# Idle matmuls on TensorE, a nested loop, a later pause with an earlier release, and another order and cut of the first loads

## The chip, the cores and the metric

One core of one Trainium2 chip runs the kernel. The metric is the device time of one execution in microseconds; three executions of the kernel before gave 162.36, 162.41 and 163.22 us, and the median, 162.41 us, is what the change is measured against. The kernel is compiled once for the fixed shapes below.

## The reference

A linear layer with a low-rank addition. x is 16 x 2048 rows of 256 floats, 32,768 rows or 33.55 MB; W is 256 x 256, lora_A 256 x 16, lora_B 16 x 256, lora_E 16 values, all fp32; the output is as large as x.

```python
x_flat = x.reshape(-1, in_dim)
y = x_flat @ W
lora_out = x_flat @ lora_A
lora_out = lora_out * lora_E
lora_out = lora_out @ lora_B
y = y + scale * lora_out
return y.reshape(batch, seq_len, out_dim).astype(np.float32)
```

## The kernel before

The small matrices are folded first: weff = W + A diag(E) B scale, in bf16, so that each row of x needs one product with weff. For this TensorE transposes lora_A against an identity that GpSimd writes (L125, L127, L153), VectorE (DVE) scales it into `ate` (L157), TensorE multiplies it with lora_B (L162), and DVE adds W and rounds (L167).

The rows of x go through the core in six chunks of `PLAN` = 48, 32, 48, 48, 48 and 32 rows per partition (128 partitions; one row per partition is 128 KiB in all, so a chunk is 6 or 4 MiB). The chunks lie in four slots of on-chip memory: chunk 4 goes into the slot of chunk 0, chunk 5 into that of chunk 1. The result is written over the chunk's input in the same slot, and stored from there.

A step is 8 rows per partition; there are NS = 32 steps: steps 0 to 5 are chunk 0, 6 to 9 chunk 1, 10 to 15 chunk 2, 16 to 21 chunk 3, 22 to 27 chunk 4 and 28 to 31 chunk 5. Each step goes through these stages, with two buffers each:

- `rounded(t)`, DVE (L141): rounds the 8 rows to bf16 into `xb`. It first waits for the chunk's load, where the step begins a piece of it.
- `transposed`, TensorE (L180): eight transposes, each of two bf16 columns at once as one fp32 word, into `ps_xt`.
- `copied(t)`, DVE (L145): copies `ps_xt` to `xt`.
- `multiplied`, TensorE (L191): 16 matmuls with weff in two halves of eight, into `ps_y[0]` and `ps_y[1]`.
- ScalarE (L214): copies each half from `ps_y` into the slot. The last half of a chunk releases the chunk's store.

DVE's order is rounded(0), the addition of weff, rounded(1), and then copied(t), rounded(t+2) for each t. TensorE's order is a loop over pairs of steps: transposed(t+1), multiplied(t). So the matmuls of a step stand behind the transposes of the next.

All large transfers are issued by SP in one queue, in this order: chunk 0's first 16 rows, W, chunk 0's other 32 rows (`PIECES`), chunk 1, chunk 2 in two pieces of 24 rows, chunk 3; then store 0 and store 1 when their chunks are computed; load 4 after store 0 has landed; load 5 after store 1 has landed (`AFTER`, L224 to L227); then stores 2, 3, 4 and 5, each when its chunk is computed. ScalarE issues the three small loads (lora_A, lora_B, lora_E).

There is one deliberate pause: `HOLD = {3: 1}` makes DVE wait, before it rounds the first step of chunk 3 (step 16), until store 1 has landed (L136 to L140).

Of the kernel before, what the change touches and what calls it, by code (L numbers as in the profile page):

```python
# [3 lines left out]

PLAN = [48, 32, 48, 48, 48, 32]

PIECES = {0: [16, 32], 2: [24, 24]}

SLOTS = [48, 32, 48, 48]
LEAD = 4  # L10
AFTER = {1: [4, 5]}

HOLD = {3: 1}

S, G = 8, 4
P = 128
# [17 lines left out]
def kernel(tc, x, W, lora_A, lora_B, lora_E, scale, out):  # L34
    nc = tc.nc
# [8 lines left out]

    steps = [(i, r) for i, b in enumerate(PLAN) for r in range(0, b, S)]
    NS = len(steps)
    assert NS % 2 == 0

    def rows_of(flat, i):
        b, r0 = PLAN[i], starts[i]  # L50
        return flat[r0:r0 + b * P, :].rearrange("(p b) k -> p b k", b=b)

    def sbuf(name, shape, dt):
        return nc.alloc_sbuf_tensor(name, shape, dt).ap()

    def psum(name, shape, dt):
        return nc.alloc_psum_tensor(name, shape, dt).ap()
# [7 lines left out]
    ate = sbuf("ate", [R, KC, P], BF16)  # L65
    weff = sbuf("weff", [P, KC, M], BF16)
    ident = sbuf("ident", [P, P], FP32)

    xb = [sbuf(f"xb{k}", [P, S, K], BF16) for k in range(2)]
    words = [t[:, :, :].rearrange("p s k -> p (s k)").bitcast(FP32).rearrange("p (s w) -> p s w", s=S) for t in xb]  # L70
# [4 lines left out]
    ps_y = [psum(f"psum_y{k}", [P, G, M], FP32) for k in range(2)]  # L75
# [4 lines left out]
    s_w, s_a, s_b, s_e = (Count(nc, f"s_{k}") for k in "wabe")  # L80

    pieces = {}
    for i, b in enumerate(PLAN):
        parts = PIECES.get(i, [b])
        pieces[i] = [(sum(parts[:j]), n) for j, n in enumerate(parts)]
    s_ld = {(i, r): Count(nc, f"s_ld{i}_{r}") for i in pieces for r, n in pieces[i]}
    s_st = [Count(nc, f"s_st{i}") for i in range(len(PLAN))]
    s_id, s_set, s_v, s_t, s_m, s_y = (
        Count(nc, k) for k in ("s_id", "s_set", "s_v", "s_t", "s_m", "s_y"))


    can_m = nc.alloc_semaphore("can_m")
# [1 line left out]
    can_y = [[nc.alloc_semaphore(f"can_y{h}_{k}") for k in range(2)] for h in range(S // G)]  # L94

    def slot(i):
        return slots[i % LEAD][:, :PLAN[i], :]

    def load(i, parts=None):
        for r, n in parts or pieces[i]:  # L100
            s_ld[i, r].by(nc.sync.dma_start(out=slot(i)[:, r:r + n, :], in_=rows_of(x_flat, i)[:, r:r + n, :]), 16)
# [4 lines left out]
    def spent(engine, count):  # L106
        engine.wait_ge(count.sem, count.total).then_inc(count.sem, -count.total)

    def take(sem):
        nc.tensor.wait_ge(sem, 1).then_inc(sem, -1)  # L110


    with tc.tile_critical(no_gpsimd_drain=True):
        load(0, pieces[0][:1])
        s_w.by(nc.sync.dma_start(out=w_sb, in_=W.rearrange("(p c) m -> p c m", c=KC)), 16)
        s_a.by(nc.scalar.dma_start(out=a_sb, in_=lora_A.rearrange("(p c) r -> p c r", c=KC)), 16)
        s_b.by(nc.scalar.dma_start(out=b_sb, in_=lora_B), 16)
        s_e.by(nc.scalar.dma_start(out=e_sb, in_=lora_E[:, None]), 16)
        load(0, pieces[0][1:])
        for i in range(1, LEAD):  # L120
            load(i)
    tc.close()
# [9 lines left out]
    def rounded(t):  # L132
        i, r = steps[t]
        if (i, r) in s_ld:
            nc.vector.wait_ge(s_ld[i, r].sem, 16)
        if i in HOLD and r == 0:  # L136

            for _ in range(10):
                nc.vector.engine_nop()
            nc.vector.wait_ge(s_st[HOLD[i]].sem, 16)  # L140
        nc.vector.tensor_copy(out=xb[t % 2], in_=slot(i)[:, r:r + S, :]).then_inc(can_t[t % 2], 1)  # L141

    def copied(t):
        nc.vector.wait_ge(s_t.sem, t + 1)
        nc.vector.tensor_copy(out=xt[t % 2], in_=ps_xt[t % 2]).then_inc(can_m, 1)  # L145


    nc.vector.wait_ge(s_b.sem, 16)
# [3 lines left out]
    for c in range(KC):  # L152
# [4 lines left out]
    s_v.by(nc.vector.tensor_scalar(  # L157
        out=ate, in0=ps_at, scalar1=e_sb, scalar2=float(scale),
        op0=mybir.AluOpType.mult, op1=mybir.AluOpType.mult))
    nc.tensor.wait_ge(s_v.sem, 2)  # L160
    for c in range(KC):
        aeb_done = nc.tensor.matmul(ps_aeb[:, c, :], ate[:, c, :], b_bf, start=True, stop=True)  # L162
    s_set.by(aeb_done)
    rounded(0)
    nc.vector.wait_ge(s_w.sem, 16)
    nc.vector.wait_ge(s_set.sem, 2)
    s_v.by(nc.vector.tensor_add(out=weff, in0=w_sb, in1=ps_aeb))  # L167
    rounded(1)
    for t in range(NS):
        copied(t)  # L170
        if t + 2 < NS:
            rounded(t + 2)

    nc.vector.sem_inc(can_t[NS % 2], 1)


    def transposed(k):
        nc.tensor.wait_ge(can_t[k], 1)
        for j in range(S):
            done = nc.tensor.transpose(ps_xt[k][:, j, :], words[k][:, j, :], ident)  # L180
            if j == 1:
                done.then_inc(can_t[k], -1)
        done.then_inc(s_t.sem, 1)

    def multiplied(k):
        take(can_m)
        for h in range(S // G):
            nc.tensor.wait_ge(can_y[h][k], 1)
            for j in range(G):
                for c in range(KC):  # L190
                    done = nc.tensor.matmul(  # L191
                        ps_y[h][:, j, :], pairs[k][:, h * G + j, :, c], weff[:, c, :],
                        start=(c == 0), stop=(c == KC - 1))
                if j == 0:
                    done.then_inc(can_y[h][k], -1)
            done.then_inc(s_m.sem, 1)

    transposed(0)
    nc.tensor.wait_ge(s_v.sem, 3)

    with nc.tensor.Fori(0, NS // 2):
        for k in range(2):
            transposed(1 - k)
            multiplied(k)
    s_t.total, s_m.total = NS + 1, NS * S // G

    for h in range(S // G):
# [1 line left out]
    n = 0  # L209
    for i, r in [(i, r + g) for i, r in steps for g in range(0, S, G)]:  # L210
        n += 1
        nc.scalar.wait_ge(s_m.sem, n)
        t, h = divmod(n - 1, S // G)
# [16 lines left out]
    for count in [s_a, s_id]:  # L230
        spent(nc.tensor, count)
    spent(nc.tensor, s_v)
    for count in [s_b, s_e, s_w, s_set, s_t] + list(s_ld.values()):
        spent(nc.vector, count)
    spent(nc.scalar, s_m)
    nc.tensor.wait_ge(can_y[0][NS % 2], 1).then_inc(can_y[0][NS % 2], -1)
# [37 lines left out]
```

## Time and profile before

| | us |
|---|---|
| median of three executions | 162.41 |
| the profiled execution | 162.57 |
| its span, first to last instruction | 161.3 |
| TensorE matmul busy | 93.2 |
| VectorE busy | 76.6 |
| ScalarE busy | 63.2 |
| mean granted TensorE clock | 0.822 of full |

An execution is 1.3 us longer than the span, which runs from the first to the last instruction that was profiled. Busy time of the compute engines counts their instructions alone. The DMA share is the mean busy share of the core's 16 DMA engines; in short windows it can pass 1.00, because a packet of up to 48 KiB is put down to the window in which it falls. The granted clock was 1.00 from the start to 22 us, about 0.5 for 3.4 us from there, 1.00 until 63 us, 0.50 through the pause and up to 90 us, 1.00 until 134.7 us, and 0.50 from then to the end, when TensorE has nothing more to do.

The pause is easy to find in the trace: ScalarE's last copy before it ends near 60.8 us, and DVE's first rounding after it begins at 83.4 us. At the start DVE rounds two steps at 9.6 and 11.3 us and then waits 5.5 us for the second piece of chunk 0, until 19.6 us. Issues to landing: chunk 0's first piece 8.4 us, W 8.5 us, the stores 28.0 to 36.5 us.

### The profile page before, as it was taken

Reading aid. Unit: us, or ns where it says so; the run is one execution under the profiler, and the core shown is the slowest. Engines: PE = TensorE matmul, PEld = TensorE weight load, DVE = VectorE, ACT = ScalarE, POOL = GpSimd, SP = SyncE. Lnnn points to the kernel's source line nnn. Section 1 sums busy time; section 2 is a strip of 40 time slices with the busy share of each in tenths; the row PEclk is TensorE's granted clock in tenths of the full one; section 3 lists DMA queues with packets and bytes.
Section 4 is the critical chain, followed back from the end, with each engine's and each line's share of the span. In section 5 each row is a group of like instructions: output and inputs, shape, how many; then the busy total and the mean of one; then the engine's idle time right before and its main releaser. Section 6 shows DMA issues by size and latency. Waiting matters only on the chain.

```text
span 161.3 us, 1875 instructions
## 1 busy us (share of the span) xinstructions
PE 93.2 (58%) x780; PEld 83.4 (52%) x780; DVE 76.6 (48%) x67; ACT 63.2 (39%) x65; POOL 0.7 (0%) x6
## 2 busy tenths in 40 slices
PE   0149179999999980000009999999999970000000
PEld 0038058999999960000008899999999960000000
DVE  0074197898989800000039589898989500000000
ACT  0300406777768680000000577776868680000000
POOL 0100000000000000000000000000000000000000
PEclk9999978999999998555555899999999997555555
DMA  4999999999999999989999989999999999999993
GB/s 137 407 496 423 423 423 433 408 463 408 506 439 427 402 390 392 500 386 398 480 435 402 500 378 406 471 431 404 463 463 415 402 451 463 427 402 402 447 447 171
DMA packets 2370, 67.42 MB, mean 418 GB/s; under 512 B 432, under 2 KB 448, under 8 KB 576
## 3 DMA queue, kind: packets, MB, share of 16 engines
q1 hardware_dynamic: 2160, 67.37, 97.7%
q10 hardware_dynamic: 208, 0.03, 0.1%
q14 instruction: 2, 0.02, 0.0%
HBM read 33.85 MB, written 33.55 MB: 418 GB/s over the span
## 4 chain that ended last, share of the span: by engine, by line
PE 44%; DMA 22%; ACT 2%; DVE 1%; issue 0%
PE psum_y L191 29%; DMA out_dram<-xy 22%; PE psum_xt L180 14%; ACT xy L214 2%; DVE xb L141 1%
## 5 line engine op out<-in xcount | busy, mean ns | idle before, releaser
L214 ACT COPY xy<-psum_y 128x1024 f32<-128x1024 f32 x64 | 61.9, 1015 | 64.0 <-PE psum_y L191 64.0
L191 PE MATMUL psum_y<-weff,xt 128*128 128x256 bf16 x512 | 64.9, 283 | 0.1
L191 PEld LDWEIGHTS psum_y<-weff,xt 128*128 128x128 bf16 x512 | 51.8, 101 | 7.6 <-issue 0.3
L141 DVE CAST xb<-xy 128x2048 bf16<-128x2048 f32 x32 | 39.0, 1217 | 32.3 <-DMA out_dram<-xy 26.8
L180 PE MATMUL psum_xt<-ident,xb 128*128 128x128 f32 x264 | 37.1, 288 | 29.7 <-DVE xb L141 29.7
L180 PEld LDWEIGHTS psum_xt<-ident,xb 128*128 128x128 f32 x264 | 32.3, 150 | 31.3 <-DVE xb L141 30.9
L145 DVE COPY xt<-psum_xt 128x1024 f32<-128x1024 f32 x32 | 39.2, 1224 | 11.2 <-PE psum_xt L180 11.2
L153 PE MATMUL psum_xt<-ident,a_sb 128*16 128x128 f32 x2 | 0.6, 397 | 6.8 <-POOL ident L127 6.8
L149 DVE CAST b_bf<-b_sb 16x256 bf16<-16x256 f32 x1 | 0.3, 281 | 7.9 <-DMA b_sb<-in_lora_B_dram 7.9
L214 ACT ACT_TABLE_LOAD x1 | 1.3, 1283 | 6.0 <-PEq L123 6.0
L153 PEld LDWEIGHTS psum_xt<-ident,a_sb 128*16 128x16 f32 x2 | 0.1, 90 | 6.7 <-DMA a_sb<-in_lora_A_dram 6.7
L162 PE MATMUL psum_xt<-b_bf,ate 16*128 16x256 bf16 x2 | 0.6, 402 | 2.4 <-DVE ate L157 2.4
L162 PEld LDWEIGHTS psum_xt<-b_bf,ate 16*128 16x128 bf16 x2 | 0.1, 104 | 2.9 <-DVE ate L157 2.9
L157 DVE TENSOR_SCALAR ate<-psum_xt,e_sb 16x256 bf16<-16x256 f32 x1 | 0.5, 473 | 1.0 <-DMA e_sb<-in_lora_E_dram 1.0
L167 DVE TENSOR_TENSOR weff<-w_sb,psum_xt 128x512 bf16<-128x512 f32 x1 | 0.7, 669 | 0.0
L127 POOL TENSOR_SCALAR_AFFINE_SELECT ident<-ident 128x128 f32<-128x128 f32 x1 | 0.3, 292 | 0.2 <-POOL ident L125 0.2
L125 POOL MEMSET ident<- 128x128 f32 x1 | 0.2, 205 | 5.4 <-POOLq L123 5.4
L255 POOL MEMSET const-bfloat16-1.0<- 128x1 bf16 x1 | 0.1, 102 | 0.0
L255 POOL MEMSET const-uint8-127<- 128x1 uint8 x1 | 0.1, 101 | 0.0
L255 POOL MEMSET const-float32-0.0<- 128x1 f32 x1 | 0.1, 98 | 0.2 <-issue 0.2
L255 POOL MEMSET const-float32-1.0<- 128x1 f32 x1 | 0.1, 98 | 0.0
## 6 DMA issues: line engine op xcount, KB each, us to landing
out_dram<-xy SPq DMA_DIRECT2D x4, 6144.0 KB, 30.6
xy<-in_x_dram SPq DMA_DIRECT2D x3, 4096.0 KB, 24.5
xy<-in_x_dram SPq DMA_DIRECT2D x2, 6144.0 KB, 39.3
out_dram<-xy SPq DMA_DIRECT2D x2, 4096.0 KB, 31.8
xy<-in_x_dram SPq DMA_DIRECT2D x2, 3072.0 KB, 36.7
xy<-in_x_dram SPq DMA_DIRECT2D x1, 2048.0 KB, 8.4
w_sb<-in_W_dram SPq DMA_DIRECT2D x1, 256.0 KB, 8.5
a_sb<-in_lora_A_dram ACTq DMA_DIRECT2D x1, 16.0 KB, 5.7
```

The source lines that it names most:

```text
L127: s_id.by(nc.gpsimd.affine_select(out=ident, in_=ident, compare_op=mybir.AluOpType.not_equal, fill=1.0, base=0, pattern=[[-1, P]], channel ...
L141: nc.vector.tensor_copy(out=xb[t % 2], in_=slot(i)[:, r:r + S, :]).then_inc(can_t[t % 2], 1)
L145: nc.vector.tensor_copy(out=xt[t % 2], in_=ps_xt[t % 2]).then_inc(can_m, 1)
L149: s_v.by(nc.vector.tensor_copy(out=b_bf, in_=b_sb))
L153: at_done = nc.tensor.transpose(ps_at[:, c, :], a_sb[:, c, :], ident)
L157: s_v.by(nc.vector.tensor_scalar(out=ate, in0=ps_at, scalar1=e_sb, scalar2=float(scale), op0=mybir.AluOpType.mult, op1=mybir.AluOpType.mult))
L162: aeb_done = nc.tensor.matmul(ps_aeb[:, c, :], ate[:, c, :], b_bf, start=True, stop=True)
L167: s_v.by(nc.vector.tensor_add(out=weff, in0=w_sb, in1=ps_aeb))
L180: done = nc.tensor.transpose(ps_xt[k][:, j, :], words[k][:, j, :], ident)
L191: done = nc.tensor.matmul(ps_y[h][:, j, :], pairs[k][:, h * G + j, :, c], weff[:, c, :], start=(c == 0), stop=(c == KC - 1))
L214: y = nc.scalar.copy(out=slot(i)[:, r:r + G, :], in_=ps_y[h])
L255: nc = _bacc.Bacc("TRN2", target_bir_lowering=False, num_devices=1)
```

## The change

It has five parts.

- **Order of the first loads.** W is issued ahead of everything else on SP, and then all of chunk 0 (two pieces of 24 rows instead of 16 and 32, W between them no more).
- **Chunk 2** is loaded in one piece of 48 rows instead of two of 24.
- **DVE's order at the start.** The addition of weff comes ahead of rounded(0) instead of behind it.
- **The pause.** It stands one step later, ahead of rounded(17) (t = NS/2 + 1), and waits for store 0 instead of store 1. When store 0 has landed, DVE raises `go` and waits for `s_warm` before it goes on.
- **TensorE.** `idle(n)` issues n fp32 matmuls of the identity with itself repeated four times (512 columns) into `ps_y[0]`, whose result nobody reads: one behind the transposes of lora_A, two behind the matmuls of lora_B, and five at the end of each half of the steps. The loop is nested, two passes over 16 steps each; at the end of a pass TensorE takes `go`, waits until `ps_y[0]` is free, runs the five and raises `s_warm`. The second pass does so at the very end.

```diff
-PIECES = {0: [16, 32], 2: [24, 24]}
+PIECES = {0: [24, 24]}
-HOLD = {3: 1}
+HOLD = 0
+WARM = 1, 2, 5
...
+    wide = ident[:, :].unsqueeze(1).to_broadcast([P, 4, P])
...
     with tc.tile_critical(no_gpsimd_drain=True):
-        load(0, pieces[0][:1])
         s_w.by(nc.sync.dma_start(out=w_sb, in_=W.rearrange("(p c) m -> p c m", c=KC)), 16)
...
-        load(0, pieces[0][1:])
+        load(0)
...
-        if i in HOLD and r == 0:
+        if t == NS // 2 + 1:
 
             for _ in range(10):
                 nc.vector.engine_nop()
-            nc.vector.wait_ge(s_st[HOLD[i]].sem, 16)
+            nc.vector.wait_ge(s_st[HOLD].sem, 16)
+            nc.vector.sem_inc(go, 1)
+            nc.vector.wait_ge(s_warm.sem, 1)
...
+    def idle(n):
+
+        last = None
+        for _ in range(n):
+            last = nc.tensor.matmul(ps_y[0][:, :2, :].rearrange("p g m -> p (g m)"), ident, wide, start=True, stop=True)
+        return last
...
+    idle(WARM[0])
     nc.tensor.wait_ge(s_v.sem, 2)
...
-    rounded(0)
     nc.vector.wait_ge(s_w.sem, 16)
     nc.vector.wait_ge(s_set.sem, 2)
     s_v.by(nc.vector.tensor_add(out=weff, in0=w_sb, in1=ps_aeb))
+    rounded(0)
     rounded(1)
...
     nc.vector.sem_inc(can_t[NS % 2], 1)
+    nc.vector.sem_inc(go, 1)
...
+    idle(WARM[1])
     transposed(0)
     nc.tensor.wait_ge(s_v.sem, 3)
 
-    with nc.tensor.Fori(0, NS // 2):
-        for k in range(2):
-            transposed(1 - k)
-            multiplied(k)
+    with nc.tensor.Fori(0, 2):
+        with nc.tensor.Fori(0, NS // 4):
+            for k in range(2):
+                transposed(1 - k)
+                multiplied(k)
+        take(go)
+        nc.tensor.wait_ge(can_y[0][0], 1)
+        idle(WARM[2]).then_inc(s_warm.sem, 1)
+    s_warm.total = 2
```

The other lines of the diff count the new semaphores and take them back to zero at the end.

More of the change, by code (lines that the diff above doesn't have):

```diff
@@ L46 @@
     NS = len(steps)
-    assert NS % 2 == 0
+    assert NS % 4 == 0
     def rows_of(flat, i):
@@ L87 @@
     s_st = [Count(nc, f"s_st{i}") for i in range(len(PLAN))]
-    s_id, s_set, s_v, s_t, s_m, s_y = (
-        Count(nc, k) for k in ("s_id", "s_set", "s_v", "s_t", "s_m", "s_y"))
+    s_id, s_set, s_v, s_t, s_m, s_y, s_warm = (
+        Count(nc, k) for k in ("s_id", "s_set", "s_v", "s_t", "s_m", "s_y", "s_warm"))
+    go = nc.alloc_semaphore("go")
     can_m = nc.alloc_semaphore("can_m")
@@ L232 @@
     spent(nc.tensor, s_v)
-    for count in [s_b, s_e, s_w, s_set, s_t] + list(s_ld.values()):
+    for count in [s_b, s_e, s_w, s_set, s_t, s_warm] + list(s_ld.values()):
         spent(nc.vector, count)
```

## The prediction

> **What bounds the kernel now.** I read the totals of the page first, then the transfers, then who waits.
>
> ```profile
> span 161.3 us, 1875 instructions
> PE 93.2 (58%) x780; PEld 83.4 (52%) x780; DVE 76.6 (48%) x67; ACT 63.2 (39%) x65; POOL 0.7 (0%) x6
> DMA  4999999999999999989999989999999999999993
> q1 hardware_dynamic: 2160, 67.37, 97.7%
> HBM read 33.85 MB, written 33.55 MB: 418 GB/s over the span
> ```
>
> No compute engine is busy for more than 58% of the span. The one queue that SP feeds (q1) keeps the 16 DMA engines busy for 97.7% of it, with a thinner first and last slice. The windows give the rate by stage (columns: stretch and its length, five engines' busy time and count, PEclk, DMA share, GB/s):
>
> ```profile
> 0.00:4.00 4.00, 0.00 (x0) 0.00 (x0) 0.00 (x0) 0.00 (x0) 0.20 (x4) 1.00 0.49 134
> 2.00:57.00 55.00, 43.03 (x349) 37.83 (x350) 37.77 (x34) 27.23 (x28) 0.50 (x2) 0.97 1.01 424
> 20.00:50.00 30.00, 29.02 (x249) 26.19 (x250) 26.56 (x23) 19.09 (x20) 0.00 (x0) 0.94 1.02 439
> 106.00:158.00 52.00, 26.15 (x240) 24.07 (x238) 19.56 (x17) 20.31 (x22) 0.00 (x0) 0.78 1.00 431
> 158.00:161.30 3.30, 0.00 (x0) 0.00 (x0) 0.00 (x0) 0.00 (x0) 0.00 (x0) 0.50 0.30 129
> ```
>
> The steady rate is about 431 GB/s (the 52 us window, whose edges blur least). The opening 22 MiB of x and 0.25 MiB of W are 23.33 MB; 55 us at 424 are 23.3 MB, so the queue reads from 2 to 57 us without a pause. Then the waits and the issue times (issue time first; L104 stores, L101 loads):
>
> ```profile
> SPq L101 <- DMA out_dram<-xy: 35.0, 2, 25.6
> DVE xb L141 <- DMA out_dram<-xy: 26.8, 1, 26.8
> 37.21 0.35 SPq L104 DMA_DIRECT2D out_dram<-xy  x1
> 47.69 0.34 SPq L104 DMA_DIRECT2D out_dram<-xy  x1
> 73.68 0.34 SPq L101 DMA_DIRECT2D xy<-in_x_dram  x1
> 83.38 0.34 SPq L101 DMA_DIRECT2D xy<-in_x_dram  x1
> 91.12 0.34 SPq L104 DMA_DIRECT2D out_dram<-xy  x1
> 107.07 0.34 SPq L104 DMA_DIRECT2D out_dram<-xy  x1
> 122.79 0.33 SPq L104 DMA_DIRECT2D out_dram<-xy  x1
> 133.27 0.33 SPq L104 DMA_DIRECT2D out_dram<-xy  x1
> ```
>
> Loads 4 and 5 are issued when stores 0 and 1 have landed (73.7 and 83.4). What is left at 83.4 is loads 4 and 5 and stores 2 to 5: 6+4+6+6+6+4 = 32 MiB = 33.55 MB, at 431 GB/s 77.8 us, and 83.4+77.8 = 161.2: the span. So nothing but the transfer of bytes sets the end. An issue matters only if it comes after the queue has run out. Running out by the same sum: 57 for store 0 (issued 37.2), 73.7 for store 1 (47.7), 83.4 for load 4 (73.7), 98.0 for load 5 (83.4), 107.7 for store 2 (91.1), 122.3 for store 3 (107.1), 136.9 for store 4 (122.8), 151.5 for store 5 (133.3). The margins lie between 9.7 us (load 4) and 26 us (store 1). The chain of waits names TensorE for 44% of the span, but only up to store 5's issue; behind it stand 18 us of backlog. It also gives the price of a step (start, length):
>
> ```profile
> 84.67 1.97 PE psum_xt L180 x8
> 86.63 3.41 PE psum_y L191 x16
> ...
> 95.47 0.87 PE psum_xt L180 x8
> 96.35 1.75 PE psum_y L191 x16
> ```
>
> At a granted clock of 0.5 a step is 5.4 us, at 1.0 it is 2.62.
>
> **The change part by part.**
>
> *W ahead of x.* The bytes are the same; the first thing in the queue is 0.25 MiB, and x is issued one issue step (0.44 us, W's on SP) later. Either x's descriptors are there when W's 0.61 us of transfer (0.262 MB at 431) is through, and nothing is lost, or the engines start a second time. The trace does not show a short transfer in front. The price of one start: the first 4 us moved 4 x 134 = 536 KB, worth 1.24 us of the steady rate, so 2.76 us went; 0.94 of it is before the first issue, leaving 1.8 us. A second start would overlap the first, x's issue being 0.44 us behind W's, so I put its bound at half, 0.9 us. Below nothing: one start that falls better, 0.2 us, half of the issue step. I take 0, since x's issue (1.38) lies well before the first data (about 2), and keep -0.2 to +0.9.
>
> *24 and 24 rows, chunk 2 in one piece.* One DMA fewer of 15. Bounds for a hand-over between queued transfers: nothing, as the window 20 to 50, with three of them (by 431 GB/s at about 27, 34 and 42), has share 1.02; at most all that 2 to 57 lacks against 431, 55 x (1-424/431) = 0.9 us over eight transfers, 0.11 us. I take 0, range -0.1 to 0. [...]
>
> *What it does to the first half.* x's first 24 rows land behind W and 1 MiB more than now: W now lands at 1.38+8.5 = 9.9, plus 2.4 us (1 MiB at 431) gives 12.3 against 9.3 for the 16 rows. Three steps instead of two are there, and the second piece still lands near 19.6 (the same bytes), so most of DVE's 5.5 us wait at L141 goes. At 2.62 us a step chunk 0 is out at about 32 to 35 (now 37.2). Chunk 2 now lands whole at about 43.4 instead of its first half near 36. DVE wants it at about 38, so the wait moves there, 5 to 6 us. Step 9's matmuls stand behind step 10's transposes on TensorE, so store 1 goes at 49 to 51 instead of 47.7. Deadlines 57 and 73.7: cost nothing; without the 22 us of cover the delay would be 1.3 to 3.3 us.
>
> *weff before the first rounding.* DVE's wait for W and for the set-up matmuls (10.3 now) moves ahead of xb 0, 0.67 us of addition with it. The rows land at 12.3, so this is covered; uncovered it would be 0.7 us.
>
> *Idle matmuls.* 1+2+5, and 5 more at the end. A plain fp32 matmul of 512 columns is not in the trace. From below: four 128-column fp32 transposes, 0.87/8 each, 0.44 us. From above: four of the slowest row (0.397 us, L153) at half clock, 3.2 us. I take 1.5, in between. The first one stands in 2.4 us in which TensorE waits for ate. Two more, 3 us, delay the first step by at most 3 from 10.3 (6 at the upper bound, store 0 then before 42 against 57). The last five end long before the last store.
>
> *The pause.* DVE now waits for store 0 (73.7), not store 1 (83.4), and one step later, so chunk 2's last step is out at about 63 to 66 and store 2 can go at 83.8, behind load 5, instead of 91.1. Behind DVE's new wait for s_warm stand the rounding of step 17 and all later ones, and TensorE behind these; five idle matmuls are 2.2 to 16 us, so step 17 begins at 77 to 91 (7.5 us taken: 82; now step 16 begins at 84.7). Steps to 21 end at about 95 and chunk 4 has to land, near 98: a new wait of 3 us, then 11 x 2.62 and 2 us of copying out: store 5 at 129 to 132 against 151.5. No issue misses its time at either bound (worst: all of it 6.3 us later than now, store 3 at 113 against 122). Cost nothing.
>
> *Sum.* 0 in the span: 161.3, in its own execution 162.57 (1.3 lies around the span); the median of the three runs is 0.16 lower, 162.41. Forecast 162.4.
>
> **The rivals.** 0.5% is 0.81 us, about what a measurement of this kernel can tell from no change; the limits are 161.6 and 163.2.
>
> Slower by a second start: W's short transfer is over before x's data flow, and the engines start twice. It decides from 0.81 us on, with a price up to 0.9: 163.3. For it: the first window at 134 GB/s; against it: only 0.44 us between the issues. Chance 0.12.
>
> Slower because the second half runs at half clock throughout: at 5.4 us a step 16 of them from 82 end at 168, copying out takes 2 and store 5 9.7 more: 180. It decides once compute is over 18 us late. Against it: the granted clock was back at 1.00 six us after the last pause. Chance 0.02.
>
> Faster by a more even start and end: the last 3.3 us moved 129 GB/s, worth 1.0 us at full rate, and the start lost up to 0.9 us beyond latency. An order of transfers that lets all 16 engines begin and finish together gets some 1.1 of these 1.9: 161.3. Against it: the last transfers, their sizes and order are unchanged. Chance 0.08.
>
> Faster by fewer hand-overs at a fixed cost each: from the rows 0.11 us, 162.3, no change. [...]
>
> That the idle matmuls do not keep the clock up, or the first half does not gain, is a rival that leaves the time at 162.4, for the margins hold; it is inside the forecast.
>
> **How the numbers follow.** Forecast 0.75, second start 0.12, half clock 0.02, even ends 0.08, hand-overs 0.03: faster 0.11, same 0.75, slower 0.14. The range takes the unknown terms, -0.3 to +0.9, around 162.4, and 0.6 more below for even ends: 161.5 to 163.4.
>
> **What would show it.** Queue q1 keeps its 67.37 MB at a share near 97.7%, its packets fall from 2160 by one transfer's 144 (2160/15) to 2016, and the window 106 to 158 keeps 431 GB/s. Stores 2 to 5 are issued earlier (2 near 84, 5 near 130), loads 4 and 5 still near 73.7 and 83.4, and the span does not follow. Wrong would be: load 4 issued over 0.8 us away from 73.7 (then the start or the first 72 us of transfer changed), an issue after its deadline, or a different rate with the same bytes.

## The result and the profile after

The changed kernel takes 162.75 us (median of 22 executions, 162.53 to 163.38) against 162.46 us for the kernel before in the same series (22, 162.23 to 163.22). The ratio is 1.0017, with a 95% interval of 1.0010 to 1.0024: 0.28 us slower. That is inside the 0.5% that the prediction counted as no change, and inside its range, but it is clear of the measurement's noise, and no loss was forecast.

First lines of the page after that answer to those of before, then three of its windows (columns as there; PE is TensorE's matmuls, PEld its weight loads, ACT ScalarE, SP the engine that issues the transfers):

```profile
span 161.6 us, 1936 instructions
PE 108.2 (67%) x806; PEld 87.8 (54%) x806; DVE 76.1 (47%) x67; ACT 63.2 (39%) x65; POOL 0.7 (0%) x6
DMA  4999999989999999989999989999999999899993
q1 hardware_dynamic: 2016, 67.37, 97.3%
```

```profile
0.00:4.00 4.00, 0.00 (x0) 0.00 (x0) 0.00 (x0) 0.00 (x0) 0.20 (x4) 1.00 0.48 153
2.00:57.00 55.00, 44.80 (x329) 35.85 (x330) 35.23 (x33) 25.01 (x26) 0.50 (x2) 0.97 1.01 425
106.00:158.00 52.00, 29.21 (x236) 24.47 (x234) 18.32 (x16) 19.27 (x20) 0.00 (x0) 0.81 1.00 433
```

The same bytes go in 2016 packets, at the same rate in the long windows. The start is not dearer: the first 4 us moved 153 GB/s, before 134. The issue times on SP (L108 stores, L105 loads):

```profile
34.51 0.35 SPq L108 DMA_DIRECT2D out_dram<-xy  x1
50.55 0.34 SPq L108 DMA_DIRECT2D out_dram<-xy  x1
73.39 0.34 SPq L105 DMA_DIRECT2D xy<-in_x_dram  x1
83.70 0.34 SPq L105 DMA_DIRECT2D xy<-in_x_dram  x1
84.08 0.43 SPq L108 DMA_DIRECT2D out_dram<-xy  x1
105.53 0.34 SPq L108 DMA_DIRECT2D out_dram<-xy  x1
121.29 0.33 SPq L108 DMA_DIRECT2D out_dram<-xy  x1
131.76 0.33 SPq L108 DMA_DIRECT2D out_dram<-xy  x1
```

Every issue is well ahead of its deadline, most of them earlier than before. The queue is never empty (DMA share 1.01 and 1.00 in the two long windows), and still the end is later. What did move is where TensorE works. The same stretch, just behind the turn of the queue from loads to stores, first of the kernel before, then of the changed kernel:

```profile
57.50:72.00 14.50, 2.18 (x20) 1.73 (x18) 0.00 (x0) 2.57 (x3) 0.00 (x0) 0.69 0.99 430
```

```profile
57.50:72.00 14.50, 7.70 (x71) 6.88 (x69) 4.08 (x4) 6.71 (x8) 0.00 (x0) 0.92 0.99 429
```

And the timeline of the changed kernel shows why (start, length, instruction group, and in brackets the wait before it):

```profile
43.51 1.23 DVE L146 CAST xb<-xy 128x2048 bf16<-128x2048 f32 x1 [5.36 <-DMA xy<-in_x_dram]
...
62.42 1.04 PE L194 MATMUL psum_xt<-ident,xb 128*128 128x128 f32 x8
...
63.29 1.91 PE L205 MATMUL psum_y<-weff,xt 128*128 128x256 bf16 x16
```

DVE waits 5.4 us for chunk 2, now loaded whole, so its steps run late; and the first half has one step more in it, step 16, which needs chunk 3. TensorE works until 65.2 us beside store 0, where it ended at 59.7 before.

### The profile page after: what moved, and what is told of

Read it like the earlier page. It is cut to its first block, busy times and chain, and to the rows that moved or that the text cites. A ratio compares the mean times of both kernels' runs of the same rounds, so it can differ in the third digit from the quotient of the medians.

```text
span 161.6 us, 1936 instructions
## 1 busy us (share of the span) xinstructions
PE 108.2 (67%) x806; PEld 87.8 (54%) x806; DVE 76.1 (47%) x67; ACT 63.2 (39%) x65; POOL 0.7 (0%) x6
## 3 DMA queue, kind: packets, MB, share of 16 engines
q1 hardware_dynamic: 2016, 67.37, 97.3%
## 4 chain that ended last, share of the span: by engine, by line
DMA 39%; PE 22%; ACT 2%; DVE 1%; issue 0%
DMA out_dram<-xy 24%; DMA xy<-in_x_dram 15%; PE psum_y L205 13%; PE psum_xt L194 7%; PE psum_y L156 3%; ACT xy L234 2%; DVE xb L146 1%
## 5 line engine op out<-in xcount | busy, mean ns | idle before, releaser
L205 PE MATMUL psum_y<-weff,xt 128*128 128x256 bf16 x512 | 63.9, 280 | 0.9 <-PEq L114 0.5
L205 PEld LDWEIGHTS psum_y<-weff,xt 128*128 128x128 bf16 x512 | 51.2, 101 | 8.6 <-issue 1.7
L194 PE MATMUL psum_xt<-ident,xb 128*128 128x128 f32 x264 | 36.1, 283 | 11.2 <-DVE xb L146 11.1
L194 PEld LDWEIGHTS psum_xt<-ident,xb 128*128 128x128 f32 x264 | 31.2, 146 | 14.8 <-DVE xb L146 14.4
L156 PE MATMUL psum_y<-ident 128*128 128x512 f32 x26 | 16.3, 776 | 8.6 <-PEq L114 8.4
L156 PEld LDWEIGHTS psum_y<-ident 128*128 128x128 f32 x26 | 6.0, 248 | 15.3 <-issue 14.7
```

What stands on the lines that cost most here:

```text
L156: last = nc.tensor.matmul(ps_y[0][:, :2, :].rearrange("p g m -> p (g m)"), ident, wide, start=True, stop=True)
L205: done = nc.tensor.matmul(ps_y[h][:, j, :], pairs[k][:, h * G + j, :, c], weff[:, c, :], start=(c == 0), stop=(c == KC - 1))
```

## The experiments

Beside the views of the profile, the packets of the trace were read one by one. A store packet of 48 KiB mostly takes 1.815 us and one of 32 KiB 1.213, on all engines, but some take up to 7% longer, in long runs in which each begins where the last ends, so on a single engine. In the table, "excess" is the sum of what store packets took beyond 1.829 or 1.213 us, counting those that are 0.021 us to 7.2% over. The 1.829, and the 1.83 of the expectations, lies 0.014 us above the usual packet, so the column is low by that for each slow one (13 of them in before: 0.2 us); the comparisons change little. One more packet in each trace is some 0.35 us too long, in store 0 with the pause of before and in store 1 with that of the change; it is not counted. "Loss" is the time at which a transfer has landed, less what the bytes up to there need at 0.302 us a row, mean over the 16 engines. "The turn" is the first one, from loads to stores near 57 us; the second, from load 5 to store 2, is near 106 us. TensorE's busy time is from the windows. Kernels named a_ are the changed kernel with an edit, b_ and t_ the kernel before with one.

```
                   PE busy, us   excess, us         loss, us                      time
kernel             57.5 to 72   57-81.5  from 107.5  to chunk 2  at turn   ratio  95% interval
before                2.2        0.06      1.19        3.43       0.52      1
b_again               3.1        0.18      1.15        3.50       0.33     0.9995 0.9979-1.0011
b_wfirst              2.4        0.00      1.09        3.05       1.04     0.9992 0.9979-1.0006
b_whole               3.5        0.06      1.27        3.33       0.49     1.0010 0.9990-1.0029
b_newloads            4.9        0.18      1.19        3.02       1.01     0.9999 0.9987-1.0011
a_oldloads            4.7        0.00      1.18        3.36       0.46     0.9996 0.9983-1.0009
a_oldloads2           5.2        0.22      1.04        3.60       0.19     1.0014 1.0005-1.0022
a_split2              4.5        0.03      1.20        3.22       0.74     1.0001 0.9986-1.0016
the changed kernel    7.7        0.30      1.18        3.20       0.84     1.0017 1.0010-1.0024
a_again               8.9        0.30      1.16        3.00       1.17     1.0001 0.9981-1.0020
a_third               7.3        0.28      1.08        3.06       0.98     1.0024 1.0014-1.0034
a_noidle              7.2        0.48      1.02        3.20       0.91     1.0018 1.0007-1.0028
a_early               1.9        0.00      0.81        3.20       0.76     0.9980 0.9972-0.9989
a_early_oldorder      5.1        0.18      0.67        3.57       0.27     0.9986 0.9977-0.9995
a_p23                 2.2        0.05      1.02        3.29       0.72     0.9987 0.9965-1.0008
a_p4                  7.4        0.30      0.87        3.05       0.98     1.0003 0.9980-1.0026
```

An excess costs time only as far as its engine is the last to end. Followed packet by packet from 107.5 us on, the slow engine is the last in 13 of the 20 traces. In the other seven the last one has no slow packet from there on, but was already the last of all at the second turn. The changed kernel is among these: its last engine ends at 161.23 us, the slow one at 160.91; in a_again it is 161.43 and 161.28. Only in a_third is the slow one last (160.95, the next 160.06). So the sums in the table say how much one engine is slowed, and not yet what a kernel loses.

**Which half of the change: the loads, or the pause with its matmuls.** Four kernels on one chip: the changed kernel again; before with the new loads (the first diff); the changed kernel with the old loads (its reverse, with chunk 2 in two pieces); and the changed kernel without idle matmuls (the second).

```diff
-PIECES = {0: [16, 32], 2: [24, 24]}
+PIECES = {0: [24, 24]}
...
-        load(0, pieces[0][:1])
         s_w.by(nc.sync.dma_start(out=w_sb, ...), 16)
...
-        load(0, pieces[0][1:])
+        load(0)
```

```diff
-WARM = 1, 2, 5
+WARM = 0, 0, 0
...
-        idle(WARM[2]).then_inc(s_warm.sem, 1)
+        nc.tensor.sem_inc(s_warm.sem, 1)
```

> The changed kernel once more, for a second trace and a second ratio. If its loss is a lasting one, the ratio to before is again about 1.002 (+0.3 us). Theory 1 (transfers disturbed between the landing of store 0 and that of store 1, where the first trace of the changed kernel has 10.3 us between the issues of loads 4 and 5 and before 9.7): again 10.2 to 10.4 us, with load 4 issued at 73.3 to 73.5. Theory 2 (the difference is where the slowest of 16 DMA engines ends, by chance of the trace): the 10.3 does not come back, while the ratio does.

> Before with only the new order and cut of the loads (W ahead, 24 and 24 rows, chunk 2 whole), pause, loop and idle matmuls as before. Theory L (the loads cost the 0.3 us, by a second start or by all engines arriving later at the turn to the stores): ratio 1.0015 to 1.0025. Theory P (pause, loop and idle matmuls cost it): 0.998 to 1.0005, with load 4 issued 0.2 to 0.3 us earlier than before (73.4), as in the changed kernel, and 9.7 us between loads 4 and 5.

> The changed kernel with the loads of before (16 and 32 rows with W between, chunk 2 in two pieces). Theory L: ratio 0.9995 to 1.0005. Theory P: 1.0015 to 1.0035, 10.2 us or more between the issues of loads 4 and 5, load 4 near 73.7.

> The changed kernel without any idle matmul (a plain semaphore increment in their place; nested loop, pause at step 17 and loads stay). Theory I (the idle matmuls disturb the transfers or pull in instructions while store 1 runs): ratio 0.999 to 1.0005, 9.7 us between loads 4 and 5. If it is the nested loop or the place of the pause instead: 1.0015 to 1.0025 and 10.3 us as in the changed kernel. Either way TensorE is at half clock at the start of the second half and store 3 goes some 3 us later, which costs nothing.

The 10.3 us between loads 4 and 5 did not come back in the second trace (74.60 to 84.28, 9.7 us), and it does not go with the loss: a_oldloads has 10.0 us and no loss, a_oldloads2, below, 9.6 and a loss. So theory 1 falls. On this chip a_again's ratio, 1.0001, told nothing (its interval reaches 1.002). Neither the loads alone (0.9999) nor the rest alone (0.9996) showed the loss. Without idle matmuls it was there in full (1.0018): they are not its cause. Store 3 did not go 3 us later there, as was expected, but 0.9 us earlier (104.65 against 105.53), since DVE had no idle matmuls to wait for (6.0 us of them in the changed kernel).

**The parts of the loads.** The kernel before again; before with W ahead; before with chunk 2 whole; and the changed kernel with chunk 2 in two pieces.

```diff
# a_split2
-PIECES = {0: [24, 24]}
+PIECES = {0: [24, 24], 2: [24, 24]}
```

> The kernel before once more: what a ratio of a kernel to itself shows (0.999 to 1.001), and a second trace of it. In the packets of the trace, mean over the 16 engines and over what its bytes need at 302 ns a row: the transfer of chunk 3, whose end is the turn from loads to stores, loses 0.4 to 0.6 us, as in the two traces with these loads so far (0.52 and 0.46); all of it from the start to the last store 4.1 to 4.3 us. Were the larger loss with the new loads (0.84 to 1.17 in four traces) chance, it would be above 0.8 here too.

> Before with W ahead of x alone (16 and 32 rows, chunk 2 in two pieces). Theory start (W ahead saves at the start, and the engines pay it back at the turn): loss up to chunk 0's landing 3.0 to 3.2 us instead of 3.27, at the turn 0.7 or more. Theory cut (chunk 2 in one piece makes the turn dear): at the turn 0.4 to 0.6. The ratio 0.999 to 1.001 by both. A second start, as in the rival of the prediction, would show over 4.0 us up to chunk 0.

> Before with chunk 2 in one piece alone. Theory cut: the turn loses 0.8 us or more, the total is 4.35 to 4.5 us, ratio 1.0005 to 1.002. Theory start: the turn as before, 0.4 to 0.6, total 4.1 to 4.25, ratio 0.998 to 1.0005.

> The changed kernel with chunk 2 in two pieces of 24 rows again. Theory cut: the turn is back at 0.4 to 0.6 us, the total near 4.1, ratio 0.998 to 1.0005 and so the loss of the change gone. Theory start: the turn keeps 0.8 us or more, ratio 1.001 to 1.0025.

In the packets theory start holds: in every trace with W ahead the engines are some 0.3 us further at chunk 2 and lose more at the turn (0.72 to 1.17 us against 0.19 to 0.52 in the table's others). Theory cut falls. But the times did not follow the turn: W ahead alone measured 0.9992, and a kernel compared with itself spread over 0.9979 to 1.0011 here, too wide for 0.2%.

**What slows packets behind the turn.** In the first trace of before, one engine's packets of 48 KiB take some 1.91 us instead of 1.815 from 108 until 131 us, as long as the core computes, and that engine is the last to end, at 160.74 us (the others end between 158.9 and 160.69). Four kernels put 24 to 25 us of work behind the last step, beside stores 3 to 5: copies of ScalarE, copies of VectorE, many small matmuls, few large ones.

```diff
# t_pesmall; t_pebig has 7 times 4 matmuls as in the change's idle(), t_act and t_dve 24 and 20 copies
+    nc.tensor.wait_ge(can_y[0][0], 1)
+    with nc.tensor.Fori(0, 14):
+        for _ in range(16):
+            nc.tensor.matmul(ps_y[0][:, 0, :], weff[:, 0, :P], weff[:, 1, :], start=True, stop=True)
```

> Before with 24 more copies of ScalarE (PSUM to a scratch tile) behind the last store's issue, about 25 us beside stores 3 to 5; the results are untouched. Theory B (one of the 16 DMA engines sends its store packets of 48 KiB in 1.91 us instead of 1.83 while the core computes, 106 to 131 us in the trace of before, and is the slowest at the end) with ScalarE as its cause: packets of 1.91 us go on to about 158, that engine ends 0.8 to 1.1 us later, ratio 1.004 to 1.007. If ScalarE is not the cause: ratio 0.999 to 1.001.

> Before with 20 more copies of VectorE (PSUM to a scratch tile) behind its last copy, about 25 us from 129 on; results untouched. VectorE as the cause of theory B: slow packets to about 155, ratio 1.004 to 1.007; otherwise 0.999 to 1.001.

> Before with 224 more bf16 matmuls of 256 columns on TensorE behind its last one (14 times 16, about 25 us); their results are not read. TensorE, or the sheer number of its instructions, as the cause of theory B: slow packets to about 157, ratio 1.004 to 1.007; otherwise 0.999 to 1.001.

> Before with 28 more fp32 matmuls of 512 columns (the idle matmul of the change, 0.85 us each at full clock) on TensorE behind its last one, about 24 us. If it is TensorE's array or its reads: ratio 1.004 to 1.007 as with the small ones. If it is the number of its instructions (eight times fewer here): slow packets of under 1.85 us and 0.999 to 1.001.

The ratios are, in this order, 1.0006 (0.9986 to 1.0027), 0.9996 (0.9967 to 1.0024), 1.0063 (1.0039 to 1.0087) and 1.0008 (0.9989 to 1.0027). Only the many small matmuls cost time, and as much as theory B said. The windows behind 132 us, of the kernel with the small and of that with the large matmuls, show as much TensorE time in both, but four times as many records of matmuls in the first (the 28 large ones, 0.85 us each, left 56):

```profile
132.00:158.00 26.00, 24.39 (x224) 21.61 (x221) 0.00 (x0) 0.57 (x1) 0.00 (x0) 1.00 0.99 426
```

```profile
132.00:158.00 26.00, 23.84 (x56) 10.26 (x54) 0.00 (x0) 0.36 (x1) 0.00 (x0) 1.00 0.99 427
```

And the same stretch of before, of the kernel with ScalarE's copies and of that with VectorE's:

```profile
132.00:158.00 26.00, 0.15 (x2) 0.00 (x0) 0.00 (x0) 1.24 (x2) 0.00 (x0) 0.55 0.99 427
```

```profile
132.00:158.00 26.00, 0.00 (x0) 0.00 (x0) 0.00 (x0) 24.97 (x25) 0.00 (x0) 0.54 0.99 429
```

```profile
132.00:158.00 26.00, 0.06 (x1) 0.00 (x0) 21.41 (x18) 1.14 (x2) 0.00 (x0) 0.55 0.98 425
```

In the packets, the excess from 107.5 us on is 2.18 us with the small matmuls, and 1.13, 1.18 and 1.24 with ScalarE's, VectorE's and the large ones, against 1.19 in before. The column leaves out packets that are only a little slow. All that packets took beyond 1.815 and 1.213 us behind 132 us (counting those 5 ns over or more) is 0.05 us in before, 0.14 with 25 copies of ScalarE, 0.16 with 18 of VectorE, 0.34 with 56 records of large matmuls and 1.16 with 224 small ones. Above before that is 3 to 6 ns for each copy or matmul record. So in these five traces it goes with the number of instructions beside stores, and not with how long an engine is busy. Where there were many, one engine took some 0.1 us more than 1.815 for 48 KiB, 5 to 6%. That it must be TensorE's instructions is not shown: the other two engines ran too few to tell. Nor were small and large matmuls alike in all but number, since their type and operands differ too.

**Taking TensorE off the stores.** If this is what the change loses by, it is the 5.5 us of TensorE's work that it moved beside store 0. Loads in smaller pieces take that back, and more. The first two below were measured on one chip with the changed kernel and a_oldloads again; the last two on another.

```diff
-PIECES = {0: [24, 24]}
+PIECES = {0: [24, 24], 2: [24, 24], 3: [24, 24], 4: [24, 24]}   # a_early
+PIECES = {0: [24, 24], 2: [24, 24], 3: [24, 24]}                # a_p23
+PIECES = {0: [24, 24], 4: [24, 24]}                             # a_p4
```

> The changed kernel with chunks 2, 3 and 4 loaded in two pieces of 24 rows each. Theory B (TensorE's instructions beside stores slow one DMA engine by 4.5%): step 16 no longer waits for the whole of chunk 3, nor step 22 for the whole of chunk 4, so TensorE's first half ends near 60 us instead of 65 and the second near 123 instead of 130; 12 us less beside stores, 0.5 us less on that engine, ratio 0.998 to 0.9995, 0.2 to 0.4 us below the changed kernel of the same call. If stores beside TensorE are not what costs the change its 0.3 us: no lower than the changed kernel, 1.0005 to 1.002.

> As the one with chunks 2, 3 and 4 in two pieces, with chunk 0 and W in the order of before too (16 rows, W, 32 rows). Theory start (with W ahead the engines are 0.2 us ahead at chunk 0 and lose 0.4 us more at the turn to the stores): turn loss 0.35 to 0.55 us in the mean, another 0.1 to 0.2 us off the time, ratio 0.9965 to 0.9985. If the order at the start does not matter: the same time as with W ahead.

> The changed kernel a third time, for a comparison on the same chip. By both theories 1.001 to 1.0025; the one slow engine takes some 1.9 us a 48 KiB packet from 59 to 66 us beside store 0 too, 0.2 to 0.3 us in all, where before has under 0.1.

> The changed kernel with the loads of before again (0.9996 the first time, interval 0.9983 to 1.0009). Theory B alone (TensorE's first half ends near 65 here too): 1.001 to 1.002. Theory start alone: 0.9995 to 1.0005. In the packets of the trace the turn loses 0.35 to 0.55 us by theory start, against 0.74 to 1.17 with W ahead.

> The changed kernel with chunks 2 and 3 in two pieces, chunk 4 whole: only the first half of TensorE's work is taken off the stores (it ends near 60 us instead of 65; step 22 still waits for all of chunk 4, second half ends near 130). Theory B: 0.2 to 0.3 us below the changed kernel, ratio 0.9995 to 1.001, so that the loss of the change is its first half beside store 0. If the gain of the version with chunks 2, 3 and 4 cut came from chunk 4 alone: 1.0015 to 1.0025.

> The changed kernel with chunk 4 alone in two pieces: the first half still ends near 65 us beside store 0, the second ends near 124 instead of 130. Theory B: 0.25 to 0.35 us below the changed kernel, ratio 0.9995 to 1.001. If the gain came from chunks 2 and 3 alone: 1.0015 to 1.0025.

a_early took 162.05 us (161.97 to 162.25) where before took 162.38 and the changed kernel 162.73: 0.33 us below the one and 0.68 below the other, more than the 0.2 to 0.4 us that theory B gave. It beats both. Two of its windows, and then its last issue from the timeline:

```profile
57.50:72.00 14.50, 1.89 (x18) 1.45 (x15) 0.00 (x0) 2.28 (x3) 0.00 (x0) 0.72 0.99 429
106.00:158.00 52.00, 22.27 (x173) 17.99 (x170) 11.90 (x11) 13.96 (x15) 0.00 (x0) 0.75 1.00 433
```

```profile
124.82 0.33 SPq L108 DMA_DIRECT2D out_dram<-xy  x1
```

TensorE is back at 1.9 us behind the turn, and has 173 matmuls beside stores 2 to 5 instead of 236. Store 5 goes 7 us earlier, which by the deadlines is worth nothing, for it waits in the queue either way; what fits the gain is the excess of the slow engine, 0.81 us in all instead of 1.36 in a_third, for in both traces this engine is the last to end (160.42 and 160.95 us). That a_early gains 0.68 us, 0.13 more than this, is not explained.

The old order at the start gave 162.22 us, not less than W ahead but more: theory start is right about the packets and wrong about the time. (In that trace the slow engine is not the last.) a_third shows the change's loss again, 1.0024. a_oldloads2 now lost 1.0014, with 0.22 us of excess behind the turn; the first run of that kernel had none and lost nothing. On the last chip the executions lay far apart (a_p23's from 162.24 to 164.03): a_p23 (0.9987, below what theory B gave) and a_p4 (1.0003) lie on the side of theory B, but the interval of a_p4 holds both answers and that of a_p23 reaches from a gain to nearly no change. So it is not shown that the first half's overlap makes the loss. Two of the three traces of the changed kernel speak against it as the whole cause, since their last engine is another: in the first that engine had the packet that is 0.35 us too long, in store 1, and lost 0.54 us at the second turn; in a_again it was already the last when chunk 3 had landed, at 59.75 us.

## Why the prediction was wrong

- *Nothing but the transfer of bytes sets the end; an issue matters only if it comes after the queue has run out.* The step that failed: the last term of the sum, the bytes that are left over a fixed 431 GB/s. The deadlines were right, and every issue kept its own. But the end is that of the slowest of 16 engines, and how long an engine took for its bytes depended on what the core did meanwhile: 224 small matmuls moved nothing in the queue and cost 0.63% (t_pesmall), and the same bytes went 0.2% faster than before in a_early. That the sum met the span, 161.2, was partly luck: it counts from 83.4 us, when store 1 was reported, but the engines had gone on to load 4 between 81.5 and 82.9. How much of the change's own 0.28 us comes from this step stays open.
- *What it does to the first half: cost nothing* and *The pause: cost nothing.* The mechanisms were read rightly: DVE's new wait for chunk 2 was given as 5 to 6 us and measured 5.36; store 1 at 49 to 51, measured 50.55; chunk 2's last step at 63 to 66, TensorE ended at 65.2; the wait for chunk 4 until about 98, measured 98.2; store 5 at 129 to 132, measured 131.76. But the late steps were priced only by the issues that they delay, not by what lies beside them. Three traces of the changed kernel have 0.28 to 0.30 us of excess behind the turn, two of before 0.06 and 0.18; from 107.5 us on it is 1.08 to 1.18 against 1.15 and 1.19. That is some 0.14 us more, and it can reach the time only where the slow engine is the last. So by these traces it is about half of the 0.28 us at most; the rest is not settled. Two sizes were off without a price: the wait for chunk 4 was given as 3 us and was 6.82, and step 17 began at 79.6 us instead of 82.
- *W ahead of x: 0, from -0.2 to +0.9.* Right in size. There was no second start: up to chunk 2 the engines lose 3.20 us instead of 3.43. The turn takes the lead back (0.84 us lost there instead of 0.52), and no effect on the time was found (b_wfirst 0.9992, interval 0.9979 to 1.0006). That 162.75 us lies within the range is luck, for only this term's +0.9 reaches so far above 162.4. (The terms give 163.3 as the upper bound; 163.4 is a slip.)
- *24 and 24 rows, chunk 2 in one piece: 0, from -0.1 to 0.* Right for the hand-over itself (b_whole 1.0010, interval 0.9990 to 1.0029). The chance of 0.03 for a gain by fewer hand-overs needs some 0.8 us for the one that goes, and no run shows such a price: a_early, with three more transfers than the changed kernel, is the fastest against before (0.9980), 0.68 us below the changed kernel.
- *Idle matmuls: 1.5 us each, from 0.44 to 3.2.* Five took 6.0 us in the pause, 1.2 each. That they cost nothing is borne out: without them the loss stayed (a_noidle, 1.0018).
- *The rivals.* A second start, half clock throughout (the granted clock was 0.92 from 86 to 130 us), more even ends and fewer hand-overs all fell. (For the even ends, the last 3.3 us were read as 1.0 us lost; that is what their bytes are worth at full rate, and 2.3 us is what was lost.) Half a per cent as what can be told from no change was too coarse: two series of 22 executions told 0.17%. Work that is hidden but slows the transfers that hide it was not among them.

## What to carry to other kernels

Where a queue of transfers is never empty, its rate is still a term of the sum (224 small matmuls beside it cost 0.63% here): ask which engines work beside which transfers, before and after, and not only whether each issue is in time. A difference of 0.2%, some 0.3 us, is less than what lay between the ends of the 16 DMA engines here (158.9 to 160.74 us in before), so look at the packets of single engines and ask which one ends last in each trace. Set a suspected cost where it shows by itself, as the extra matmuls did, instead of hunting it in the noise. A load cut into pieces can pay for its hand-overs by letting work begin, and so end, earlier, as in a_early (162.05 us, the changed kernel 162.73).

## What the runs showed of the hardware

- Where many instructions ran beside stores, one DMA engine was slow: 1.91 us instead of 1.815 for 48 KiB beside 240 matmuls in 26 us (before, 106 to 132 us), and 1.16 us of slow packets in all beside 224 small matmuls (t_pesmall, behind 132 us) against 0.05 in before. On loads beside TensorE no such runs of packets appear in the traces of before and of the changed kernel: from 84.5 to 103.5 us no load packet is as much as 15 ns too long (13 ns at most). It is not the time in which an engine works: ScalarE copied for 24.97 of 26 us (t_act) and added 0.09 us of slow packets. By what path the instructions act is open. Each execution of the experiments comes with a span and a granted clock, so all were recorded, and no run shows whether the effect is there without the recording.
- At the first turn from loads to stores the engines lose 0.2 to 1.2 us in the mean, at the second (106 us) about 0.1. In the traces of before and of the changed kernel those that are ahead lose the most there; in a_again the one that was last lost 2.0 us, and it ended last. The cause was not tried.
